# Cutting GpSimd's subtractions into pieces of 256 columns in a two-layer diffusion trunk

## Chip, cores and metric

The kernel runs on one core of a Trainium2 chip. The metric is the device time of one execution, in microseconds. TensorE (PE) does the matrix products, VectorE (DVE), ScalarE (ACT) and GpSimd (POOL) the elementwise work, and SyncE (SP) issues the DMAs.

## What is computed

The reference is two layers of a transformer backbone on 512 latent tokens and 256 context tokens of width 1024, in float32. Each layer does this (cut to what matters here):

```
h = modulate(rms_norm(x, g_mix_pre[l]), mod[:, 0], mod[:, 1])
p = h @ w_in[l]                      # four groups of attention heads read slices of p
y = concatenate([ya, yb, ym, yd], axis=-1) @ w_out[l]
x = x + mod[:, 2, None] * rms_norm(y, g_mix_post[l])
f = conv_ffn(modulate(rms_norm(x, g_ffn_pre[l]), mod[:, 3], mod[:, 4]), ...)
x = x + mod[:, 5, None] * rms_norm(f, g_ffn_post[l])
# conv_ffn: u = depthwise_conv(h @ w_up) ; (silu(a) * v) @ w_down, 2 x 2816 wide
```

The context tokens go through the same layer, but their last layer is not needed, so the second layer has only 512 rows behind the projections.

## The kernel before

Every large product is made of three: each float32 operand is held as a high part, rounded to TensorE's narrower fp32r format, and a low part, the operand minus its high part. `mm3` multiplies high by high, high by low and low by high into one PSUM bank. The function `split` makes the two parts: ScalarE copies the operand into the high tile (L249), and then GpSimd or VectorE subtracts (L250). Which of the two it is, is the argument `eng`.

GpSimd subtracts for almost all the weights (`weights`, tiles `wr` to `wh` and `wl`, 128 x 1024), for the gated FFN activations (`gh`, `gl`: 770 columns in the first layer, 512 in the second), for rotated queries and keys (`hilo`, tile `f`: 768 or 512 columns), for some early blocks of 256 columns (`hc`), and for half of the normalized blocks (`by_feature`, tile `m`; these operands have three dimensions). VectorE subtracts for the rest, most of it out of PSUM.

The stages of a layer follow one another: projections and attention (`mix`), whose heads run in an order that is written out by hand (`ORDER`); the output product (`wout`); and the FFN (`ffn_main`), a loop over 22 blocks of 128 hidden columns in groups of 3 or 4. A block has two up-products into PSUM (tile `up`, two buffers of the pool `A`), each followed by the depthwise convolution (ScalarE L1221, VectorE L1222 and L1224, which read that PSUM and so set when the buffer is free again), the SiLU on ScalarE (L1228), the product of gate and value on VectorE (L1229), and the split. The down-products (`dn`) of a group come behind it.

In the first layer's FFN, VectorE also makes the modulation vectors of later stages, row by row: 56 weight tiles `wm`, multiplied by the conditioning vector and summed (L497), with two SBUF inputs of 1024 columns. `rsqrt` is a Newton iteration on VectorE, a chain of dependent instructions with 1 to 12 columns (L282 to L292).

Instructions stand in program order, but the order on each engine is planned by the library when the kernel is built: it lists what is ready by a simulated timeline (`schedule_with_timeline_sim`), so other lengths or counts of instructions can give another order. On the chip each engine takes its instructions in the planned order.

Of the kernel before, what the change touches and what calls it, by code (L numbers as in the profile page):

```python
# [11 lines left out]
F32 = mybir.dt.float32  # L12
F32R = mybir.dt.float32r
AF = mybir.ActivationFunctionType
ALU = mybir.AluOpType
# [220 lines left out]
class Prog:  # L236
# [10 lines left out]

    def split(self, src, hi, lo, eng):
        self.nc.scalar.activation(out=hi, in_=src, func=AF.Copy)  # L249
        eng.tensor_tensor(out=lo, in0=src, in1=hi.bitcast(F32), op=ALU.subtract)  # L250

    def weights(self, src, cols, pool=None, tags=("wh", "wl"), bufs=2, eng=None, raw="wr"):
        nc = self.nc
# [1048 lines left out]
```

## Time and profile before

| | us |
|---|---|
| median of 3 runs | 1975.7 (1970.12 to 1979.73) |
| profiled execution | 1973.07 |
| its span on the core | 1971.3 |
| TensorE busy in it | 1805.3 (92%) |
| VectorE busy | 1135.2 (58%) |
| ScalarE busy | 905.0 (46%) |
| GpSimd busy | 838.5 (43%), 559 instructions |
| mean granted TensorE clock | 0.966 of full speed |

The span is the time from the first to the last instruction; 1.8 us of the profiled execution lie outside it. Busy time of an instruction includes time in which it has started and is held up inside the engine.

### The profile page before, as it was taken

The numbers are of one execution on the slowest core, as the hardware profiler recorded it, in microseconds if no ns is written. First come the engines' busy times: TensorE is split into PE (matmuls) and PEld (weight loads), VectorE is DVE, ScalarE is ACT, GpSimd is POOL, SyncE is SP. The second block draws the span as 40 slices with busy tenths as digits, with TensorE's granted clock in tenths as the row PEclk, the third lists the DMA queues.
The fourth block names the chain that finished last, engine by engine and source line by source line (L and its number), as shares of the span: only waits on it lengthen the run. The fifth ranks groups of instructions, "written<-read, shape, count | busy, mean of one in ns | idle before, by whom it ended". The sixth has DMA issues, their size and how long they took to land. (4 is left out here: it accounts for less than half of the span.)

```text
span 1971.3 us, 26510 instructions
## 1 busy us (share of the span) xinstructions
PE 1805.3 (92%) x9834; PEld 1530.0 (78%) x9834; DVE 1135.2 (58%) x2119; ACT 905.0 (46%) x1597; POOL 838.5 (43%) x559
## 2 busy tenths in 40 slices
PE   6889899898988899999999977888899899999997
PEld 3878778776877788888888866777777788888885
DVE  5466877875769755454432675776786632323235
ACT  5455567875542323231313363554787444333332
POOL 1363534543234334242424434544454145545553
PEclk8999899999998999999999998989999989999999
DMA  8663452544345324242312136524253323222322
GB/s 313 185 191 108 113 172 84 174 110 148 112 173 190 118 75 161 85 150 107 118 43 86 53 130 156 128 65 119 65 150 118 119 86 98 96 96 96 107 86 85
DMA packets 76160, 239.97 MB, mean 122 GB/s; under 512 B 11136, under 2 KB 12672, under 8 KB 73216
## 3 DMA queue, kind: packets, MB, share of 16 engines
q1 hardware_dynamic: 76032, 238.28, 38.5%
q8 instruction: 78, 1.28, 0.3%
q14 instruction: 50, 0.41, 0.1%
HBM read 201.94 MB, written 36.31 MB: 121 GB/s over the span
## 5 line engine op out<-in xcount | busy, mean ns | idle before, releaser
L250 POOL TENSOR_TENSOR wl<-wr,wh 128x1024 fp32r<-128x1024 f32 (+1 forms) x178 | 440.2, 2482 | 499.7 <-ACT wh L249 478.6
L249 ACT ACTIVATE wh<-wr 128x1024 fp32r<-128x1024 f32 (+1 forms) x186 | 193.2, 1049 | 383.7 <-PE up L264 182.5
L1222 DVE SCALAR_TENSOR_TENSOR ut<-up,pc,ut 128x769 f32<-128x769 f32 (+1 forms) x84 | 74.1, 883 | 333.6 <-ACT ut L1221 333.6
L263 PE MATMUL up<-hx,wh 128*128 128x512 f32 x672 | 262.8, 391 | 0.0
L264 PE MATMUL up<-hx,wh 128*128 128x512 f32 x672 | 262.5, 391 | 0.0
L265 PE MATMUL up<-hx,wl 128*128 128x512 f32 x672 | 262.2, 390 | 0.0
L820 PE MATMUL s<-op 128*128 128x256 f32 (+4 forms) x648 | 160.2, 358 | 34.2 <-ACT P L837 18.3
L250 DVE TENSOR_TENSOR ptl<-tp,pth 128x512 fp32r<-128x512 f32 (+1 forms) x208 | 136.2, 663 | 40.7 <-ACT pth L249 39.6
L820 PEld LDWEIGHTS s<-op 128*128 128x128 f32 (+1 forms) x648 | 110.8, 198 | 56.8 <-ACT P L837 28.3
L265 PEld LDWEIGHTS up<-hx,wl 128*128 128x128 f32 x672 | 126.4, 188 | 27.1
L263 PEld LDWEIGHTS up<-hx,wh 128*128 128x128 f32 x672 | 126.5, 188 | 25.6
L264 PEld LDWEIGHTS up<-hx,wh 128*128 128x128 f32 x672 | 126.5, 188 | 25.1
L1127 PE MATMUL dn<-wh,gh 128*128 128x512 f32 x440 | 140.3, 398 | 4.6 <-ACT gh L249 4.2
L865 POOL TENSOR_SCALAR P<-P,st 128x768 f32<-128x768 f32 (+2 forms) x120 | 95.9, 801 | 114.1 <-DVE st L841 84.5
L1127 PE MATMUL dn<-wl,gh 128*128 128x512 f32 x440 | 139.3, 396 | 0.0
L889 PE MATMUL tp<-ident,P 128*128 128x128 f32 x800 | 127.9, 280 | 12.2 <-DVE P L863 6.8
L1127 PE MATMUL dn<-wh,gl 128*128 128x512 f32 x440 | 138.0, 398 | 0.0
L249 ACT ACTIVATE pth<-tp 128x512 fp32r<-128x512 f32 (+1 forms) x208 | 116.6, 576 | 38.2 <-PE tp L889 36.7
L837 ACT ACTIVATE P<-s,st 128x768 f32<-128x768 f32 (+2 forms) x120 | 94.1, 786 | 79.2 <-DVE st L828 35.0
L497 DVE SCALAR_TENSOR_TENSOR wm<-wm,cb 128x1024 f32<-128x1024 f32 x56 | 107.1, 1925 | 31.4 <-DMA wm<-wmod 31.1
L828 DVE TENSOR_REDUCE st<-s 128x1 f32<-128x768 f32 (+2 forms) x120 | 95.6, 808 | 50.7 <-PE s L820 49.7
L896 PE MATMUL po<-ptl,vt 128*128 128x256 f32 x400 | 112.3, 303 | 13.2 <-DVE ptl L250 13.2
(286 smaller groups left out, 4326.5 us busy)
## 6 DMA issues: line engine op xcount, KB each, us to landing
wr<-wup SPq DMA_DIRECT2D x88, 512.0 KB, 3.8
wm<-wmod SPq DMA_DIRECT2D x56, 512.0 KB, 5.0
wr<-wdn SPq DMA_DIRECT2D x44, 512.0 KB, 3.8
op<-sc SPq DMA_DIRECT2D x36, 384.0 KB, 5.4
wr<-win SPq DMA_DIRECT2D x26, 512.0 KB, 4.3
wk<-wmk SPq DMA_DIRECT2D x12, 1024.0 KB, 6.9
op<-sc SPq DMA_DIRECT2D x60, 192.0 KB, 5.6
wm<-wm SPq DMA_DIRECT2D x8, 1024.0 KB, 9.4
```

The costliest lines, as they stand in the source:

```text
L249: self.nc.scalar.activation(out=hi, in_=src, func=AF.Copy)
L250: eng.tensor_tensor(out=lo, in0=src, in1=hi.bitcast(F32), op=ALU.subtract)
L263: mm(ps, lh, rh, start=first, stop=False)
L264: mm(ps, lh, rl, start=False, stop=False)
L265: mm(ps, ll, rh, start=False, stop=last)
L497: nc.vector.scalar_tensor_tensor(out=j, in0=raw, scalar=1.0, in1=cb[v], op0=ALU.mult, op1=ALU.mult, accum_out=self.mods[l][:, ch, f, v:v + 1])
L820: nc.tensor.matmul(full[:, o:o + w], q[:rows, qcol:qcol + P], k[:rows, c0:c0 + w], start=i == 0, stop=i == len(passes) - 1 and not msk)
L828: nc.vector.tensor_reduce(out=nm, in_=ps[:, :nk], axis=AX.X, op=ALU.max, negate=True)
L865: nc.gpsimd.tensor_scalar(out=a[:, :nk], in0=a[:, :nk], scalar1=ra, scalar2=1.0, op0=ALU.mult, op1=ALU.mult)
L889: nc.tensor.transpose(tp[:, a * 256 + j * P:a * 256 + (j + 1) * P], ptile[j][:, pos[kt]:pos[kt] + P], self.ident)
L896: nc.tensor.matmul(po[:, :256], vw, t[:, a * 256:(a + 1) * 256], start=n == 0, stop=n == total - 1)
L1127: mm(ps[:, c], a, b[:, c], start=first and i == 0, stop=last and i == 2)
```

## The change

The subtraction of `split` is issued as one instruction per 256 columns where GpSimd does it and the operand has two dimensions. A 1024-column operand gets four instructions, 770 columns get three and one of 2 columns, 768 three, 512 two; 256 columns and three-dimensional operands stay one. VectorE's subtractions and ScalarE's copies stay as they are.

```
     def split(self, src, hi, lo, eng):
         self.nc.scalar.activation(out=hi, in_=src, func=AF.Copy)
-        eng.tensor_tensor(out=lo, in0=src, in1=hi.bitcast(F32), op=ALU.subtract)
+        n = src.shape[-1]
+        step = 256 if eng is self.nc.gpsimd and len(src.shape) == 2 else n
+        for o in range(0, n, step):
+            c = slice(o, min(n, o + step)) if step < n else slice(None)
+            a, b, d = (src[:, c], hi[:, c], lo[:, c]) if step < n else (src, hi, lo)
+            eng.tensor_tensor(out=d, in0=a, in1=b.bitcast(F32), op=ALU.subtract)
```

## Rows read from the trace of the kernel before

**Rows 1.** The page: busy time by engine, and the chain by engine.
```profile
PE 1805.3 (92%) x9834; PEld 1530.0 (78%) x9834; DVE 1135.2 (58%) x2119; ACT 905.0 (46%) x1597; POOL 838.5 (43%) x559
...
PE 28%; DVE 5%; ACT 2%; issue 2%; DMA 2%; POOL 1%; SPq 0%; ACTq 0%; POOLq 0%; DVEq 0%
```

**Rows 2.** Busy time by stage; columns as in its first line.
```profile
core 0: us, PE busy (x) PEld busy (x) DVE busy (x) ACT busy (x) POOL busy (x), PEclk, DMA share, GB/s
...
108.00:470.00 362.00, 330.97 (x2175) 285.90 (x2174) 271.48 (x626) 243.61 (x550) 175.48 (x182) 0.96 0.45 133
...
570.00:720.00 150.00, 135.53 (x692) 115.80 (x692) 128.96 (x147) 45.79 (x50) 62.28 (x24) 0.94 0.43 150
...
1120.00:1520.00 400.00, 340.47 (x2076) 296.84 (x2075) 286.15 (x627) 242.74 (x491) 184.44 (x154) 0.95 0.41 112
...
1600.00:1971.30 371.30, 357.24 (x1550) 291.42 (x1549) 119.74 (x170) 130.66 (x164) 186.44 (x89) 0.98 0.29 97
```

**Rows 3.** Waits of PE: who for whom, us in total, times, longest.
```profile
PE up L263 <- DVE ut L1224: 14.3, 6, 4.5
PE po L896 <- DVE ptl L250: 13.2, 20, 2.8
...
PE dn L1127 <- ACT gh L249: 4.2, 2, 3.3
...
PE up L265 <- POOL wl L250: 0.7, 1, 0.7
```

**Rows 4.** Groups of POOL by shape: count, busy us, mean ns, idle before.
```profile
L250 POOL TENSOR_TENSOR wl<-wr,wh 128x1024 fp32r<-128x1024 f32 x174 | 433.4, 2500 | 495.9 <-ACT wh L249 478.0 <-issue 9.0 <-DMA wr<-wout 5.9
...
L250 POOL TENSOR_TENSOR gl<-ut,gh 128x770 fp32r<-128x770 f32 x22 | 41.8, 1901 | 66.6 <-ACT gh L249 66.6
...
L250 POOL TENSOR_TENSOR f<-p,f 128x768 fp32r<-128x768 f32 x14 | 27.1, 1936 | 15.5 <-ACT f L249 15.4
...
L250 POOL TENSOR_TENSOR hx<-m,hx 128x512 fp32r<-128x512 f32 x12 | 15.4, 1282 | 88.2 <-ACT hx L249 88.1
...
L250 POOL TENSOR_TENSOR hc<-op,hc 128x256 fp32r<-128x256 f32 x4 | 3.0, 752 | 8.0 <-ACT hc L249 8.0
```

**Rows 5.** Timelines of DVE, POOL and ACT, 602 to 621: start, us, instruction.
```profile
605.39 3.15 DVE L1229 TENSOR_TENSOR ut<-ut 128x770 f32<-128x770 f32 x1
608.47 3.43 DVE L497 SCALAR_TENSOR_TENSOR wm<-wm,cb 128x1024 f32<-128x1024 f32 x1
...
611.82 2.86 DVE L497 SCALAR_TENSOR_TENSOR junk<-wm,cb 128x1024 bf16<-128x1024 f32 x1
...
614.71 1.01 DVE L1222 SCALAR_TENSOR_TENSOR ut<-up,pc,ut 128x769 f32<-128x769 f32 x1
...
604.60 6.21 POOL L250 TENSOR_TENSOR wl<-wr,wh 128x1024 fp32r<-128x1024 f32 x2 [6.66 <-ACT wh L249]
610.77 2.83 POOL L250 TENSOR_TENSOR gl<-ut,gh 128x770 fp32r<-128x770 f32 x1
...
619.18 0.85 ACT L1228 ACTIVATE ut<-ut 128x770 f32<-128x770 f32 x1 [9.75 <-DVE ut L1224]
```

**Rows 6.** L497: count, then ns minimum/median/maximum of one.
```profile
L497 DVE SCALAR_TENSOR_TENSOR wm<-wm,cb x56: 1205/1226/3427, 571.3 to 965.2; 128x1024 f32<-128x1024 f32 x56
```

**Rows 7.** Timelines of POOL and DVE, 1559.5 to 1568.7.
```profile
1560.69 4.75 POOL L250 TENSOR_TENSOR wl<-wr,wh 128x1024 fp32r<-128x1024 f32 x2 [3.74 <-ACT wh L249]
...
1560.71 2.38 DVE L288 SCALAR_TENSOR_TENSOR rs_w<-rs_y,rs_v 128x1 f32<-128x1 f32 x1
1563.13 2.33 DVE L292 SCALAR_TENSOR_TENSOR rs_y<-rs_w,rs_y 128x1 f32<-128x1 f32 x1
1565.49 0.22 DVE L288 SCALAR_TENSOR_TENSOR rs_w<-rs_y,rs_v 128x1 f32<-128x1 f32 x1
```

**Rows 8.** The chain that ended last, 1190 to 1520: start, us, what.
```profile
1216.83 0.69 DVE u L635
...
1259.20 1.90 DVE u L635
...
1338.18 1.29 POOL f L250
```

## Prediction

> **What bounds the kernel now.** I read the page first. TensorE is busy for 1805.3 of 1971.3 us, GpSimd for 838.5, and the chain that ended last has only 1% on GpSimd [rows 1]. So at most the 166 us in which TensorE stood still can be won, and the change works on an engine that is seldom the last to finish. The second view is the table by stage [rows 2]. In the second layer's FFN (1600 to 1971) TensorE is busy 357.24 of 371.3 us: little to win. It loses 362.0 - 330.97 = 31.0 us in the first layer's mix, 400.0 - 340.47 = 59.5 us in the second's, and 150.0 - 135.53 = 14.5 us in the first 150 us of the first layer's FFN, where VectorE is busy 128.96 of 150 us. The third view is TensorE's waits [rows 3]: a weight's low part ends almost none (0.7 us, once), but VectorE ends several: 14.3 us for L1224, which frees the PSUM of an up-product, and 13.2 us for `ptl`. If the change matters, it is through VectorE.
>
> The timelines show how. From 604.60 GpSimd subtracts two weight tiles back to back in 6.21 us and then `gl` in 2.83 us. In the same time three VectorE instructions, all with two SBUF inputs, take 3.15, 3.43 and 2.86 us [rows 5]. L497 alone takes 1205 ns at least and 1226 in the median [rows 6], so over 2 us of the 3.43 are waiting. Clearest is a chain of one-column instructions: L288 starts 0.02 us behind two back-to-back weight subtractions, takes 2.38 us and ends at 1563.09, where the first half of their 4.75 us is over; L292 takes 2.33 us and ends with the second; the next L288, with GpSimd idle, takes 0.22 us [rows 7]. So a VectorE instruction with two SBUF inputs waits for a GpSimd instruction that was there before it, however small it is itself, and is let in at the boundary between two GpSimd instructions. The converse shows too: two weight subtractions that at the mean take 5.0 us [rows 4] took 6.21 where L1229 and L497 went in between [rows 5].
>
> **The change, part by part.** *Count.* Of the 1024-column subtractions 174 become 696, of the 770-column ones 22 become 88; with the few of 512 and 768 columns 246 instructions become 903, and GpSimd goes from 559 to 1216.
>
> *Price of a piece.* Proportional to the columns it is 2500 / 4 = 625 ns; the 256-column subtraction that the kernel has took 752 ns [rows 4]. A line through 512 and 1024 columns, 1282 and 2500 ns, gives 673 ns. I take 0.70 us, with 0.625 and 0.752 as bounds. A 1024-column split then takes 2.8 us instead of 2.5, one of 770 columns 2.1 us and a scrap of two columns (between nothing and a whole piece) instead of 1.90. GpSimd gains 174 x 0.3 = 52 us and some 13 us for the rest, so about 65 us of busy time (with 752 ns, 174 x 0.51 + 15 = 104 us). At 838.5 us of 1971 that is hidden by its idle time: 495.9 us stand ahead of the weight subtractions alone [rows 4], and TensorE waited for a weight's low part once. In the last FFN, GpSimd's 186.44 us of 371.3 become some 210 [rows 2]. If that cover were gone, each of 88 up-products would start 0.3 us late, 26 us in all.
>
> *What VectorE gets back in the first layer's FFN.* Where an instruction with two SBUF inputs waited for the rest of a split, it now waits at most for one piece. At 605.39 three of them took 614.71 - 605.39 = 9.3 us, with L1222 right behind them. Undisturbed they take at most 3 x 1.21 = 3.6 us; with one piece ahead of each, 3.6 + 3 x 0.70 = 5.7 us. So L1222 and L1224 come 3.6 us earlier, and TensorE's longest wait for L1224, 4.5 us, shrinks by four fifths. L1222's input was there: ScalarE had done nothing for 9.75 us when L1224 released it at 619.18 [rows 5]. I carry this over as three quarters of the 14.3 us and of the 3.3 us for `gh`, which stands behind L1229 in the same queue [rows 3]: 0.75 x 17.6 = 13 us. The bounds are nothing, if another step of the same queue is late then, and all 17.6.
>
> *Clock.* [...] I count 4 us as returned, between 0 and 9.
>
> *The two mixes.* On the chain L635 took 1.90 us at 1259.20 and 0.69 us at 1216.83 [rows 8]: 1.2 us of waiting, of which a piece leaves 0.70. Such waits are scattered, and much of the 13.2 us for `ptl` is not of this kind, since `ptl` reads PSUM and only queues behind such instructions. I take 3 us for both layers, with 0 and 10 as bounds.
>
> *The norms behind the second output product.* L288 and L292 took 4.71 us [rows 7]. In pieces the two weights keep GpSimd there for 5.6 us, and the four remaining instructions of the chain each wait for a piece: 4 x 0.70 and twice (0.22 + 0.16) is 3.6 us, against 4.71 + 0.38 = 5.1. That gives 1.5 us; I count 1.
>
> *What it costs.* A `hilo` split stands between the rotation and the DMA to scratch, in front of attention; one is on the chain with 1.29 us [rows 8]. In pieces it takes 3 x 0.70 - 1.94 = 0.2 us longer [rows 4], and more if VectorE goes in between. There are 24 of them. I count 2 us; the upper bound is in the rivals.
>
> *Sum.* 13 + 4 + 3 + 1 - 2 = 19 us. The profiled execution took 1973.07 us, so it would take 1954. It lies 2.6 us under the median of the runs shown; the median would be 1975.7 - 19 = 1956.7, rounded to 1957.
>
> **The rivals.** *Nothing measurable.* VectorE's lateness is real, but the planned order puts L1222 and L1224 behind other things (two L497 stood between them in the case above), or the plan that the library makes for 657 more instructions gives back elsewhere what is won. Then a few us remain either way: 1966 to 1985. For it speaks that GpSimd has 1% of the chain [rows 1], against it that the largest single stall of the FFN is exactly this wait.
>
> *Slower, by `hilo`.* The door opens both ways: between two pieces VectorE can go first, and GpSimd waits. A split of 768 columns has two such openings; with L635's 0.69 us [rows 8] in each it ends 0.2 + 1.4 = 1.6 us later, one of 512 columns about 0.8 us. For 17 and 7 of them that is 33 us if all are on the path; half of that with nothing won in the FFN gives 1975.7 + 16 = 1992. It decides from about 10 us of such lateness beyond the gain. Against it: in the mixes GpSimd is busy less than half of the time, 175.48 of 362 and 184.44 of 400 us [rows 2].
>
> *The door doesn't open.* If adjacent pieces ran without a gap for VectorE, its instructions would wait for all four, 2.8 us instead of 2.5, and the 17.6 us would grow by an eighth, 2 us, with 2 us of `hilo`: 1980, within the no-change band. The boundary at 1563.1 speaks against it: the two subtractions there ran back to back, 4.75 us for two, and still L288 got through between them [rows 7]. [...]
>
> **How the numbers follow.** A measurement of this kernel can tell about 0.5% from no change, 9.9 us. My forecast, clearly faster, has 0.62; nothing measurable, with the shut door in it (0.05), has 0.27; slower, by `hilo` or by an unlucky plan, 0.11. The forecast's own range goes from all bounds at their best, 17.6 + 9 + 10 + 1.5 = 38 us, so 1938, up to 1965. For 8 in 10 the range must reach into the no-change case: 1939 to 1978. Faster 0.62, within 0.5% 0.27, slower 0.11.
>
> **What would show it.** GpSimd should have some 1216 instructions with a mean of 0.65 to 0.75 us for a piece (more where VectorE goes in between), and 60 to 110 us more busy time. The longest L497, 3.43 us, should fall to about 2. TensorE's wait for L1224 should fall from 14.3 us under 6 us, and the clock from 570 to 720 rise to 0.97 or more. L288 and L292 should no longer show 2.3 us beside weight subtractions. The prediction is wrong if these waits fall and the span does not (the order or ScalarE sets the stalls), if they don't fall (the door is shut), or if TensorE waits longer for scratch in the mixes.

## The result and the profile after

The changed kernel takes 1949.45 us (median of four runs, 1948.09 to 1952.87), the kernel before on the same chip 1972.91 (1967.75 to 1979.73). The ratio is 0.9873 with the interval 0.9847 to 0.9898, some 25 us by it (23.5 by the two medians). The span of the profiled execution fell by 23.5 us, from 1971.3 to 1947.8 us. Lines of `split` and behind it stand five lower in the listing after (L250 is L255, L497 is L502, L1224 is L1229).

The page of the changed kernel: busy time by engine, the chain that ended last by engine, and the largest group of GpSimd.

```profile
PE 1809.6 (93%) x9834; PEld 1534.7 (79%) x9834; DVE 1085.1 (56%) x2119; ACT 905.4 (46%) x1597; POOL 995.0 (51%) x1216
...
PE 54%; DVE 7%; ACT 3%; issue 2%; POOL 2%; DMA 1%; SPq 0%; ACTq 0%; POOLq 0%; DVEq 0%
...
L255 POOL TENSOR_TENSOR wl<-wr,wh 128x256 fp32r<-128x256 f32 x706 | 568.4, 840 | 399.2 <-ACT wh L249 379.3
```

Beside [rows 1]: VectorE executes the same 2119 instructions in 50 us less, since busy time counts the time in which an instruction is held up (2.38 us beside GpSimd against 0.22 for the L288 of [rows 7]). GpSimd has 657 instructions and 156 us more; a piece of a weight's split takes 840 ns in the mean.

The waits of TensorE after (us in total, times, longest), which answer to [rows 3]:

```profile
PE s L825 <- ACT P L842: 12.2, 20, 1.9
PE po L901 <- DVE ptl L255: 9.8, 19, 1.3
...
PE dn L1132 <- ACT gh L249: 5.4, 3, 3.8
PE dn L1132 <- POOL gl L255: 5.3, 2, 3.0
...
PE s L825 <- DMA op<-sc: 4.5, 2, 2.6
...
PE up L268 <- DVE ut L1229: 0.4, 1, 0.4
```

The wait for L1224 (L1229 now), 14.3 us, is down to 0.4. A wait for `gl` has come in, which did not exist, and the wait for `gh` has not fallen (4.2 before, 5.4 after).

The same place of the first layer's FFN as in [rows 5], on VectorE, GpSimd and TensorE (start, us, instruction):

```profile
590.88 1.50 DVE L502 SCALAR_TENSOR_TENSOR wm<-wm,cb 128x1024 f32<-128x1024 f32 x1
...
592.32 1.75 DVE L502 SCALAR_TENSOR_TENSOR junk<-wm,cb 128x1024 bf16<-128x1024 f32 x1
...
594.00 1.48 DVE L1234 TENSOR_TENSOR ut<-ut 128x770 f32<-128x770 f32 x1
595.40 1.75 DVE L502 SCALAR_TENSOR_TENSOR wm<-wm,cb 128x1024 f32<-128x1024 f32 x1
...
588.89 19.39 POOL L255 TENSOR_TENSOR wl<-wr,wh 128x256 fp32r<-128x256 f32 x14
608.24 5.19 POOL L255 TENSOR_TENSOR gl<-ut,gh 128x256 fp32r<-128x256 f32 x4
...
612.35 2.36 PE L1132 MATMUL dn<-wh,gl 128*128 128x512 f32 x4 [3.01 <-POOL gl L255]
```

The prediction's picture of a door, at which VectorE waits while a GpSimd instruction runs and is let in at the boundary to the next, holds in this stretch: no VectorE instruction waits longer than for what is left of one piece (1.75 us against 1.2 undisturbed; 3.43, 3.15 and 2.86 us before). It opens for both sides: 14 pieces need 19.39 us, 1.38 us each, since VectorE goes in between, and the three pieces and the scrap of `gl` need 5.19 us. TensorE then stands 3.01 us for `gl`. L502 over the whole program, with columns as in [rows 6] (minimum, median, maximum in ns):

```profile
L502 DVE SCALAR_TENSOR_TENSOR wm<-wm,cb x56: 1209/1514/1760, 564.9 to 945.3; 128x1024 f32<-128x1024 f32 x56
```

The longest fell from 3427 to 1760 ns, while the median rose from 1226 to 1514: more instructions wait, each for less.

The door doesn't open at every boundary, though. In attention a one-column instruction of VectorE with two SBUF inputs (0.13 us at least, 0.20 in the median) was kept out over all four pieces of a split and ended just behind them:

```profile
227.34 2.33 DVE L845 TENSOR_TENSOR st<-st 128x1 f32<-128x1 f32 x1 [0.21 <-ACT st L844]
...
226.83 2.82 POOL L255 TENSOR_TENSOR wl<-wr,wh 128x256 fp32r<-128x256 f32 x4
```

Of the 185 instructions of VectorE with two tensor inputs that took over 0.3 us longer than the shortest of their kind, three waited past the end of a GpSimd instruction. So it is the exception with 256 columns; with 128 it is not (e4).

The stages, before and after. The windows start where TensorE has its first scores, its first output product or its first down-product of the layer: the first mix, the first FFN, the second mix, and the second output product with the norms and projections up to the FFN.

```profile
82.80:463.00 380.20, 347.09 (x2267) 299.77 (x2268) 281.23 (x642) 250.20 (x564) 181.58 (x185) 0.96 0.47 138
589.40:1138.10 548.70, 533.82 (x2735) 454.05 (x2736) 299.23 (x357) 155.36 (x177) 212.81 (x90) 0.98 0.31 108
1213.40:1517.10 303.70, 265.62 (x1656) 233.75 (x1657) 226.31 (x480) 190.98 (x401) 141.90 (x130) 0.95 0.40 104
1517.10:1613.70 96.60, 85.73 (x422) 73.44 (x422) 48.80 (x111) 45.41 (x70) 33.88 (x17) 0.91 0.35 117
```

```profile
85.50:456.00 370.50, 342.84 (x2260) 297.38 (x2260) 268.80 (x642) 250.69 (x565) 195.02 (x251) 0.97 0.49 141
579.40:1119.10 539.70, 530.15 (x2736) 451.74 (x2737) 269.92 (x356) 155.93 (x178) 292.45 (x341) 0.99 0.32 110
1191.90:1490.40 298.50, 265.77 (x1649) 233.30 (x1650) 217.66 (x476) 191.85 (x401) 151.16 (x178) 0.95 0.40 107
1490.40:1590.80 100.40, 91.86 (x422) 78.77 (x421) 47.63 (x112) 46.19 (x71) 43.13 (x51) 0.85 0.34 114
```

The first FFN is 9.0 us shorter, the first mix 9.7, the second mix 5.2. The second output product is longer: 100.4 us at a clock of 0.85; before it took 96.6 us at 0.91. The forecast had the gain in the FFN, and 3 us for both mixes.

### The profile page after: what moved, and what is told of

It is laid out like the page before. It is cut to its first block, busy times and chain, and to the rows that moved or that the text cites. A ratio compares the mean times of both kernels' runs of the same rounds, so it can differ in the third digit from the quotient of the medians.

```text
span 1947.8 us, 27218 instructions
## 1 busy us (share of the span) xinstructions
PE 1809.6 (93%) x9834; PEld 1534.7 (79%) x9834; DVE 1085.1 (56%) x2119; ACT 905.4 (46%) x1597; POOL 995.0 (51%) x1216
## 4 chain that ended last, share of the span: by engine, by line
PE 54%; DVE 7%; ACT 3%; issue 2%; POOL 2%; DMA 1%; SPq 0%; ACTq 0%; POOLq 0%; DVEq 0%
PE dn L1132 14%; PE up L268 9%; PE up L270 9%; PE up L269 9%; PE s L825 2%; PE wo L1132 2%; PE po L901 1%; PE tp L894 1%; DVE rs_w L293 1%; PE pj L268 1%; PE pj L269 1%; PE pj L270 1%; DVE rs_y L297 1%; DVE ptl L255 1%; DVE acc L587 1%
## 5 line engine op out<-in xcount | busy, mean ns | idle before, releaser
L255 POOL TENSOR_TENSOR wl<-wr,wh 128x256 fp32r<-128x256 f32 x706 | 568.4, 840 | 399.2 <-ACT wh L249 379.3
L255 DVE TENSOR_TENSOR ptl<-tp,pth 128x512 fp32r<-128x512 f32 (+1 forms) x208 | 136.1, 663 | 37.0 <-ACT pth L249 35.6
L255 POOL TENSOR_TENSOR gl<-ut,gh 128x256 fp32r<-128x256 f32 (+1 forms) x132 | 91.7, 722 | 75.9 <-ACT gh L249 74.1
L901 PE MATMUL po<-ptl,vt 128*128 128x256 f32 x400 | 112.4, 303 | 10.5 <-DVE ptl L255 9.8
L901 PE MATMUL po<-pth,vt 128*128 128x256 f32 x400 | 115.2, 304 | 7.0 <-ACT y L906 5.7
```

What stands on the lines that cost most here:

```text
L255: eng.tensor_tensor(out=d, in0=a, in1=b.bitcast(F32), op=ALU.subtract)
L901: nc.tensor.matmul(po[:, :256], vw, t[:, a * 256:(a + 1) * 256], start=n == 0, stop=n == total - 1)
```

## The experiments

Each ratio is to the kernel before on the same chip; the changed kernel's is 0.9873. Only e9, e10 and e12 hold the planned order fixed; each of the others has a plan of its own. Stages and waits are those of one profiled execution of each kernel.

**Only the count of pieces (e1, e2).** As many instructions as the change, but all except one are slivers of 16 columns, ahead of the rest or behind it (of 1024 columns three of 16 and one of 976).

```
+        k = (n - 1) // 256 if eng is self.nc.gpsimd and len(src.shape) == 2 else 0
+        ends = [16 * i for i in range(1, k + 1)] + [n]        # e1
+        ends = [n - 16 * i for i in range(k, 0, -1)] + [n]    # e2
```

> [...] If the gain comes from the shorter hold (the door): the waits of L497 stay near 2.1 us, the wait of TensorE for L1224 stays above 8 us, and the time stays with the kernel before, 1965 to 1982. If it comes from the new plan that a larger number of instructions gives: a gain like that of the changed kernel is as likely as not, and the two uneven kernels differ from each other by 10 us or more.

> The same with the 16-column pieces behind (976, 16, 16, 16). Door: as the kernel before, 1965 to 1982, within some 5 us of the kernel with the small pieces in front. Plan: anything from 1940 to 1985, without relation to the other one.

e1 took 1970.59 us (0.9971, 0.9957 to 0.9985), e2 1961.13 (0.9933, 0.9909 to 0.9956). TensorE's wait for L1229 was 5.9 and 2.5 us. The hold is hardly shorter, as meant: the longest L502 is 3.30 and 3.31 us. Still the wait fell below the 8 us that e1's expectation had, and e2 is faster than before. So neither is a control without effect; whether by the boundary that a sliver adds or by its plan, they can't tell (in e10, whole splits in another order, the wait is 7.9 us). And two kernels that differ by the place of slivers alone lie 9.5 us apart, half of the gain I had forecast. That raised the question which e9 and e10 answer: what does the planned order do by itself?

**The size of a piece (e3, e4).** `step = 512` and `step = 128` in place of 256.

> Pieces of 512 columns: the longest hold is 1.25 us. Door: the mean wait of L497 lies between those of the kernel before (0.68 us over its minimum) and of the changed one (0.3 us), and the time between the two, 1955 to 1964. Plan: no order among 1024, 512 and 256 columns.

> Pieces of 128 columns: a hold of some 0.4 us each. Door: VectorE waits still less, but one weight split can now be interrupted seven times by L497 (7 x 1.2 us in the first FFN), and each piece has its fixed cost, so GpSimd's busy time passes 1150 us; I expect 1942 to 1962, that is no further gain of more than 6 us, with TensorE's waits for gl growing beyond 5.3 us. Plan: no order.

e3: 1967.56 us (0.9970, 0.9953 to 0.9986), slower than the expected 1955 to 1964. e4: 1991.04 us (1.0078, 1.0055 to 1.0102), slower than before and far outside the expected range. In e3's profiled execution, the slowest of its ten, the first FFN took 535.2 us, shorter than with 256 columns, and the mixes more than before (389.4 and 311.2 us). The wait of TensorE for `gl` in e4, and GpSimd's largest group:

```profile
PE dn L1132 <- POOL gl L255: 18.0, 4, 6.0
```

```profile
L255 POOL TENSOR_TENSOR wl<-wr,wh 128x128 fp32r<-128x128 f32 x1412 | 683.3, 527 | 327.8 <-ACT wh L249 311.5 <-issue 7.2 <-PE s L825 2.2
```

Half a piece still takes 527 ns in the mean, and `gl`, now in seven instructions, comes so late that TensorE waits 18.0 us for it. The door also stays shut more often. Twice in the first FFN a VectorE instruction (undisturbed 1.2 and 1.0 us) waited for the end of a whole run of 16 adjacent pieces, over nine boundaries:

```profile
633.98 5.27 DVE L502 SCALAR_TENSOR_TENSOR wm<-wm,cb 128x1024 f32<-128x1024 f32 x1
...
631.42 6.74 POOL L255 TENSOR_TENSOR wl<-wr,wh 128x128 fp32r<-128x128 f32 x16
...
723.71 4.90 DVE L1234 TENSOR_TENSOR ut<-ut 128x770 f32<-128x770 f32 x1
...
721.09 6.70 POOL L255 TENSOR_TENSOR wl<-wr,wh 128x128 fp32r<-128x128 f32 x16
```

Counted as for the changed kernel, 22 of e4's 91 late instructions waited past a boundary, 18 of them past five or more. Why VectorE gets in at one boundary and not at another isn't settled. How much of e4's loss is its plan isn't either.

**One place alone (e5, e6).** Pieces only in the first layer's FFN, or everywhere but there. The flag is set in `ffn_main` of the first layer and cleared behind its loop.

```
+        step = 256 if self.ffn0 and eng is self.nc.gpsimd and len(src.shape) == 2 else n
```

> Pieces only inside the first layer's FFN loop (its weights and gl); all other splits whole. Door, as predicted: this stretch brings 13 us by the waits and 4 us by the clock, so 15 to 20 us of the 23 us, 1953 to 1958. If the gain is spread over the mixes instead: 1964 to 1970.

> Pieces everywhere but in the first layer's FFN loop. Door: the rest, 3 to 8 us, 1965 to 1970, with TensorE's wait for L1224 as before, above 10 us. If the gain is in the mixes: 1953 to 1960.

e5: 1960.98 us (0.9921, 0.9903 to 0.9939), 16.6 us under the kernel before on its chip, wait for L1229 (L1231 there) 0.4 us. e6: 1949.28 us (0.9852, 0.9825 to 0.9879), with that wait untouched:

```profile
PE up L268 <- DVE ut L1231: 15.2, 7, 5.3
```

e6 is as fast as the whole change, and outside both of its expectations, although the stall on which the forecast rests is all there. The parts, 1.48% and 0.79%, add to 2.27%, the whole is 1.27%: they don't add. Two stages of e6, the first FFN and the second output product, show where:

```profile
579.90:1130.20 550.30, 534.16 (x2735) 453.94 (x2736) 295.76 (x357) 155.47 (x177) 213.91 (x96) 0.98 0.31 107
1501.30:1589.60 88.30, 80.32 (x422) 68.09 (x421) 47.63 (x112) 44.89 (x70) 40.50 (x47) 0.96 0.37 128
```

The first FFN is about as long as before, 10.6 us longer than in the changed kernel. The second output product is 12.1 us shorter than there, and nearly all of that is clock: TensorE is busy for 80.32 us at 0.96 against 91.86 at 0.85, with the same 422 products; busy time times clock is 77.1 and 78.1 us.

**One kind of operand alone (e7, e8).** Pieces only for `weights`, or for all but `weights` (an argument of `split`).

> Pieces for weights only; gl and f are whole again. [...] If the cut of gl and f carries the gain: 1960 or more.

> Pieces for gl and f only, weights whole. Door: the waits of L497 behind wl stay, so 1966 to 1978. If f in front of attention is what gains or loses: a difference from before of more than 8 us.

e7: 1956.51 us (0.9891, 0.9868 to 0.9913). e8: 1969.88 (0.9961, 0.9946 to 0.9976), the wait for L1229 9.5 us. The weights carry most of it; that is as forecast, but again with the plan in it, and e7 is slower than the 1944 to 1952 us that I had put down for it. Leaving `gl` whole brought TensorE's wait for it down from 5.3 to 3.5 us, where I had expected under 3, and the total is no better than the changed kernel's.

**Pieces and plan taken apart (e9, e10).** The program is built twice. From the first build each engine's order is read; in the second, order-only dependencies tie each instruction to the one that stood ahead of it, so that the order is that of the first. e9 has pieces in the order planned for the kernel before, e10 whole splits in the order planned for the changed kernel.

```
+    for key in order:
+        for i in by.get(key, ()):
+            e = str(i.engine)
+            if e in last:
+                tc.add_manual_dep(i, last[e].name, info(), reason="order")
+            last[e] = i
...
+    nc, names = build(arrays, False)       # e10: True
+    order = planned(names, nc)
+    nc, _ = build(arrays, True, order)     # e10: False
```

In the traces each engine of e9 takes its operations in the order of the kernel before, and each engine of e10 in that of the changed kernel; the two orders differ on every engine. The kernel before rebuilt in its own order was not run, so what the added dependencies do by themselves isn't shown.

> The pieces of the changed kernel, but every engine takes its instructions in the order that was planned for the kernel before (the pieces of a split stand together where the whole split stood). Door: the shorter hold works in any order, so most of the gain is here, 1953 to 1962, TensorE's wait for L1224 falls from 14.3 us under 5 us, and both mixes get shorter by 3 to 8 us each. Plan: no gain but in the FFN waits, 1968 to 1980.

> Whole splits, but every engine takes its instructions in the order that was planned for the changed kernel. Door: little or no gain, 1966 to 1982, with VectorE's waits as long as before. Plan: the order alone brings half of the gain or more, 1950 to 1962.

| | whole | pieces |
|---|---|---|
| order of before | 1 | e9: 0.9945 (0.9932 to 0.9959) |
| order of after | e10: 0.9917 (0.9902 to 0.9932) | 0.9873 (0.9847 to 0.9898) |

Of some 25 us the pieces alone give 0.0055 x 1973 = 11, the order alone 0.0083 x 1973 = 16. The sum, 27, is near the whole. e9 lies between its two expectations, and its mixes did not get shorter; e10 lies where the plan was to bring it. The stages of e9, and then of e10 (first mix, first FFN, second mix):

```profile
84.30:467.00 382.70, 349.99 (x2266) 302.17 (x2267) 270.85 (x643) 250.12 (x564) 192.21 (x250) 0.95 0.47 137
590.50:1127.80 537.30, 525.89 (x2735) 448.42 (x2736) 269.65 (x357) 155.95 (x177) 289.97 (x341) 0.99 0.32 110
1201.10:1512.40 311.30, 275.29 (x1656) 242.76 (x1657) 220.58 (x480) 191.06 (x401) 152.70 (x178) 0.92 0.39 103
```

```profile
83.20:454.90 371.70, 343.14 (x2259) 297.17 (x2258) 273.63 (x642) 250.12 (x564) 182.75 (x185) 0.97 0.49 142
580.00:1124.10 544.10, 530.02 (x2736) 450.90 (x2737) 296.84 (x357) 155.56 (x178) 216.46 (x90) 0.99 0.31 108
1199.60:1499.80 300.20, 267.92 (x1648) 234.45 (x1649) 219.09 (x476) 191.20 (x401) 140.45 (x130) 0.95 0.40 106
```

Pieces alone shorten the first FFN by 11.4 us and lengthen the mixes by 2.5 and 7.6; e9's profiled execution is the slowest of its six (1967.93 us, median 1963.76), so this is its less favourable side. The order alone shortens the mixes by 8.5 and 3.5 and the FFN by 4.6. One thing that the order does can be named: TensorE's wait for operands from scratch. The rows of before, e9 and e10, one each:

```profile
PE s L820 <- DMA op<-sc: 15.6, 4, 7.8
```

```profile
PE s L830 <- DMA op<-sc: 12.5, 3, 5.6
```

```profile
PE s L830 <- DMA op<-sc: 6.2, 3, 3.5
```

With whole splits and the new order it is down to 6.2 us, with pieces and the old order it stays at 12.5. TensorE's wait for L1224 falls either way, more by the pieces (e9, then e10):

```profile
PE up L273 <- DVE ut L1234: 2.6, 2, 1.4
```

```profile
PE up L273 <- DVE ut L1234: 7.9, 5, 2.1
```

**More pieces (e11, e12).** GpSimd's 1024-column additions (L588 of the changed kernel) and its three-dimensional splits are cut as well, the latter in two. e11 gets its own plan; e12 keeps the order of the changed kernel on every engine.

```
+        if eng is self.nc.gpsimd and not flat:
+            for o in (0, 2):
+                eng.tensor_tensor(out=lo[:, o:o + 2], in0=src[:, o:o + 2], in1=hi[:, o:o + 2].bitcast(F32), op=ALU.subtract)
...
-        eng.tensor_tensor(out=dst, in0=dst, in1=x, op=ALU.add)
+        step = 256 if eng is nc.gpsimd else D
+        for o in range(0, D, step):
+            eng.tensor_tensor(out=dst[:, o:o + step], in0=dst[:, o:o + step], in1=x[:, o:o + step], op=ALU.add)
```

The reason is what is left of [rows 7] in the changed kernel. The one-column instructions of the Newton chains no longer take 2.3 us beside weights, but three of them do beside a whole addition on GpSimd, one of them here:

```profile
1128.06 2.33 DVE L293 SCALAR_TENSOR_TENSOR rs_w<-rs_y,rs_v 128x1 f32<-128x1 f32 x1
```

```profile
1127.56 2.82 POOL L588 TENSOR_TENSOR acc<-acc,xr 128x1024 f32<-128x1024 f32 x1 [1.36 <-DVE rs_v L290]
```

> The changed kernel, and GpSimd's 1024-column additions behind the FFN norms (line 583 before) and its three-dimensional splits also go in pieces of 256 columns. In the changed kernel the Newton chains still wait up to 2.2 us for such an addition, about ten times. Door: 3 to 8 us less than the changed kernel, 1942 to 1948. Plan: anything within 12 us of it on either side.

> The same extra pieces as in the run before (GpSimd's 1024-column additions and its three-dimensional splits, 40 instructions more), but every engine keeps the order that was planned for the changed kernel. If the extra 13 us there came from VectorE's instructions no longer waiting for those additions and splits, this run is again some 8 to 13 us faster than the changed kernel: 1936 to 1942 us, and the one-column instructions that took 2.33 us beside a whole addition take under 1 us. If they came from the other plan and the clock behind it, this run stays within 4 us of the changed kernel: 1945 to 1953 us, although those one-column instructions are shorter. My estimate from the rows of the changed kernel: the waits beside additions and three-dimensional splits that could matter are 2.33, 1.53, 1.31, 1.25, 1.19 and 1.06 us, about 7 us of excess in all, not all of it on the path, so the second is likelier.

e11: 1936.18 us (0.9809, 0.9795 to 0.9823), below its expected range, e12: 1940.13 us (0.9816, 0.9789 to 0.9844). Both beat the kernel before and the changed one. I had thought the plan the likelier cause; with the order held fixed the gain is still 0.9873 - 0.9816, some 11 us, though the two intervals all but touch. So the extra pieces make it, in part by way of the clock, and nothing measurable is left for e11's plan. The longest of those one-column instructions is 1.2 us in e12, where under 1 was expected:

```profile
L300 DVE SCALAR_TENSOR_TENSOR rs_w<-rs_y,rs_v x108: 205/219/1206, 478.8 to 1929.8; 128x1 f32<-128x1 f32 x108
```

Where it lies: the second output product with what follows it, in e12,

```profile
1484.00:1579.50 95.50, 85.43 (x422) 72.54 (x421) 47.40 (x112) 46.16 (x71) 42.97 (x55) 0.91 0.35 120
```

takes 95.5 us at 0.91, against 100.4 at 0.85 in the changed kernel. TensorE is busy for 85.43 us with the same 422 products, against 91.86, and busy time times clock is 77.7 and 78.1 us: all of these 4.9 us are clock. Another 4.8 us lie between the first FFN's first down-product (578.2 us in e12, 579.4 in the changed kernel) and the second layer's first scores (1185.9 and 1191.9), 2.3 of them behind the last down-product, where the addition stands.

## Why the prediction came out right, and by which steps

The verdict, the mechanism and the range held: 1949.45 us against 1957 (1939 to 1978). But the total came out by two effects, and only one was in the sum.

*The door.* Right for most boundaries, and as an account of the changed kernel the rival of a shut door is out: the longest L502 fell from 3.43 to 1.76 us, and beside eight pieces the one-column L293 and L297 took 0.65 to 0.74 us each, where L288 and L292 had taken 2.38 and 2.33. The excess of that L502 over its minimum, 0.55 us, is below a piece of 0.74. Adjacent pieces did not keep VectorE out here: 14 of them were spread over 19.39 us with VectorE between them. But the door did stay shut over four pieces once in attention, and over longer runs with 128 columns (e4); the prediction drew its rule from two places in the trace, and it is no rule without exceptions.

*Wait for L1224.* Forecast under 6 us, measured 0.4; with the old order 2.6 (e9). The new order alone brings 14.3 down to 7.9 (e10).

*The term of the first FFN, 13 + 4 us.* Over-sized: 9.0 us in the changed kernel, 11.4 in the old order. The 17.6 us of waits became 10.5: L1229 0.4 us, `gh` 4.8 in this stretch, where the forecast had three quarters of its 3.3 won back, and `gl` 5.3. So 7.1 us came back and not 13. The step that failed is the cover of `gl`. I costed its pieces as GpSimd's busy time hidden by idle time. But `gl` stands at the end of a dependent chain, and each boundary in it is a turn for VectorE: 5.19 us where its four instructions undisturbed are 3 x 0.74 + 0.19 = 2.4 (medians after; the scrap by its minimum). TensorE pays 5.3 us for it. The clock from 570 to 720 is 0.95, not 0.97, and gives back 1.5 us (0.01 x 150) instead of 4. The 4 us were my estimate, and no run shows what a shorter stall gives back in clock. The trace after shows three stretches at a low clock: in windows of 1 us it is 0.50 from 602 to 608, from 613 to 615 and from 691 to 694, and TensorE had waited 3.84 us for `gh` until 603.52 and 3.01 and 2.33 us for `gl` until 612.35 and 689.61. The stretch as a whole:

```profile
570.00:720.00 150.00, 139.50 (x705) 118.19 (x704) 109.99 (x140) 42.50 (x46) 100.08 (x92) 0.95 0.40 141
```

*The price of a piece and GpSimd's busy time.* Undisturbed a piece takes 742 ns (median), near the upper bound of 752 and above the 700 taken. With the turns it is 840 in the mean. So GpSimd gained 156 us and not 65, nor the 104 of the bound. That this cost so little on the weights is as forecast: TensorE's wait for a weight's low part in an up-product, 0.7 us before, is not among the waits of the changed kernel, and reaches 3.9 us only with 128 columns.

*The two mixes, 3 us.* Mis-sized, and with the wrong cause. They gave 9.7 + 5.2 = 14.9 us, of which the order alone gives 8.5 + 3.5 = 12.0; the pieces alone lose 10.1. `ptl`, which reads PSUM, was not held up itself: none of its 208 subtractions took over 0.70 us, before or after (median 0.68). The loss by the pieces is clock for the most part: in the second mix TensorE is busy for 275.29 us at 0.92 with the products that took 265.62 at 0.95. What lowered the clock there isn't shown. The rival "slower, by `hilo`" needed TensorE to wait longer for scratch, and that wait fell in e9 too, from 15.6 to 12.5 us: nothing shows it.

*The norms behind the second output product, 1 us.* The chain beside the weights got shorter as forecast, but the stage with it got longer, 100.4 us against 96.6: TensorE's busy time rose by 6.1 us at a clock of 0.85 instead of 0.91. The sum had the clock in the first FFN alone.

*The plan.* I counted a new plan only as something that might take the gain back. By the ratios it is worth more than the pieces, 16 us against 11 (the two intervals touch), and it came out on the good side by luck. Nothing in the trace of before could tell that. The forecast of 19 us is nearer to the measured 25 than its reasoning deserves: by the door alone it would have been 11.

What stays open: which of the moved instructions brings the mixes' gain beyond the wait for scratch, and what sets the clock in the second output product, by which e6 makes good what it lacks in the first FFN.

## What to carry to other kernels

Look for short VectorE instructions with two SBUF inputs that end when a GpSimd instruction ends. Here GpSimd's instruction length was VectorE's latency (2.38 us instead of 0.22 for one column), and cutting it brought the longest L502 from 3.43 to 1.76 us. It cost little where TensorE did not wait for the cut result (a weight's low part in an up-product: 0.7 us of waiting before, none after): cut what has slack first (weights, a residual's addition). `gl`, at the end of a dependent chain, paid 5.19 us instead of 2.4 for its turns; that sparing it makes the whole faster is not shown (e7). Try the size: 128 columns lost what 256 won (1.0078 against 0.9873), each in a plan of its own. And where a library plans the order, a change of instruction count can also be a change of plan, here worth 16 us (e10): hold the order fixed in both directions before crediting the edit.

## What the runs showed that I had not expected

Pieces and VectorE instructions with two SBUF inputs took turns at most boundaries while both had work: beside the 14 pieces that took 19.39 us VectorE started ten instructions of 770 or 1024 columns. A piece of 0.74 us then takes 1.38, and an L502 of 1.2 us up to 1.76. At some boundaries VectorE wasn't let in (three of its 185 late instructions waited past one), and with pieces of 128 columns it waited past nine of them.

The new plan of an unchanged computation moved the time by 0.83% (e10), and the place of 16-column slivers, with the plan that it brings, by 0.4% (e1 against e2).

One stage's length went with its granted clock and not with its stalls: the second output product took 100.4 us at 0.85 in the changed kernel, 95.5 at 0.91 in e12 and 88.3 at 0.96 in e6. TensorE waited 2.83 us there for L587 in the changed kernel and 2.59 in e12, and 1.97 and 1.96 for `hx`; e6 has the changed kernel's stalls to 0.1 us (2.5, 2.0 and 2.8). So the length of these stalls alone doesn't set the clock, and what does isn't settled.
